# The first norm's sums of squares, taken along the turned tokens instead of by channel

## The chip, the cores and the metric

The kernel runs on one core of one Trainium2 chip. The metric is the device time of one execution in microseconds (us), the median of several. A core has TensorE (PE, with its weight loads shown apart as PEld), VectorE (DVE), ScalarE (ACT), GpSimd (POOL) and SyncE (SP), which here issues all transfers. Each engine runs its own instructions in order; between engines they wait on semaphores.

## The reference

A two-layer diffusion transformer over 512 latent and 256 context tokens of 1024 channels. Layer 0 mixes tokens by pooling, layer 1 by attention; both are followed by a squared-ReLU MLP. The change touches only the first norm, of layer 0:

```python
def rms_norm(x, g):
    xf = x.astype(jnp.float32)
    y = xf * lax.rsqrt(jnp.mean(xf * xf, axis=-1, keepdims=True) + EPS)
    return (y * g.astype(jnp.float32)).astype(x.dtype)
...
        a_l = modulate(rms_norm(h_lat, norm_g[i, 0]), sh1, sc1)
            a_c = modulate(rms_norm(h_ctx, norm_g[i, 0]), csh1, csc1)
            y_l = pool_mix(a_l, pool_w[j], pool_scale[j])
```

So for each of the 768 tokens a sum of 1024 squares is needed, then its inverse root, before the token can be pooled with its neighbours. The vectors sh1 and sc1 come from a product of the conditioning vector with `ada_w`, a weight of 24 MB per layer.

## The kernel before, in words

The tokens lie in memory with channels on the 128 partitions: `h_lat` (8 channel tiles x 512 tokens) and `h_ctx` (8 x 256). Both arrive as four pairs of channel tiles, latent and context in turn (lines 100 to 102). Behind them on SP's one queue come four 512 KB pieces of `ada_w` (`praw`, block 2), the pool weights `pw` (1 MB), four more pieces (`w`, block 4; lines 112 to 116), and then, as buffers come free, the pieces of the other blocks.

Lines 584 to 607 are the first norm. For each pair of channel tiles PE turns the tokens (transposes, L591) into PSUM; ACT copies the latent half (L597) and DVE the context half (L594) into `turned_m_hi` and `turned_m_lo`, where tokens lie on partitions. Next to that, and independent of it, ACT squares the unturned `h_lat` and `h_ctx` (`squares`, L263 and L266) and DVE adds the squares up by channel tile (L267). When all eight tiles are in, `rstd_cols` (lines 276 to 287) lets PE add over the partitions by products with a column of ones (L282), first for the latents, then for the context. DVE turns the sums into a variance (L284), POOL raises it to the power -0.5 (L286). Last, ACT and DVE scale three of the six turned token tiles each (L605, L607).

PE's order is written by hand from line 582 on. Behind the norm stand, in this order: `ada0_products(2)` (L187, on `praw`), the first pooled tile (L627, on the scaled tokens), `ada0_done(2)` (transposes L196, on ACT's copy L190 of the products), the second pooled tile, `ada0_products(4)` (L187 again, on `w`), the third pooled tile, `ada0_done(4)`, the fourth pooled tile and the first products of the pooling mixer (`mix`, L654). `ada0_done(2)` yields the scale `am` (DVE, L199 to L155), which ACT needs for `scaled` (L638); on ACT follow the rounding of `pw` (L86) and L190 of block 4. The order of ACT and DVE in this stretch is chosen by the framework's scheduler, until line 702.

After about 100 us the MLPs and the attention follow, for the rest of the time; nothing in them is edited.

Of the kernel before, what the change touches and what calls it, by code (L numbers as in the profile page):

```python
# [8 lines left out]
F32 = mybir.dt.float32  # L9
F32R = mybir.dt.float32r  # L10
AF = mybir.ActivationFunctionType
ALU = mybir.AluOpType
AX = mybir.AxisListType

P = 128
D = 1024
# [10 lines left out]
EPS = 1e-6  # L27
# [20 lines left out]
def dit_block_kernel(ctx: ExitStack, tc: tile.TileContext, xT, cols, adab, adaw, w1, w2, wqkv, wo,  # L48
                     poolw, gvec, rope, edge, eye, out):
    nc = tc.nc  # L50
    act, dve, pool, pe = nc.scalar, nc.vector, nc.gpsimd, nc.tensor

    def sb(stack, name, bufs):
        return stack.enter_context(tc.tile_pool(name=name, bufs=bufs))
# [6 lines left out]
    sc = sb(ctx, "sc", 4)  # L61
    sm = sb(ctx, "sm", 4)
# [11 lines left out]
    def new(p, shape, dt, tag, bufs=None):  # L74
        uid[0] += 1
        kw = {"bufs": bufs} if bufs else {}
        return p.tile(shape, dt, tag=tag, name=f"{tag}{uid[0]}", **kw)

    def ps_mm():
        return new(mm, [P, 1024], F32, "mm")  # L80

    def ps_aux():
        return new(aux, [P, 512], F32, "aux")
# [38 lines left out]
    neghalf = const.tile([P, 8], F32, tag="neghalf", name="neghalf")  # L122
# [117 lines left out]
    def hs(k0, k1, c0, n):  # L240

        if c0 < SEQ:
            return h_lat[:, k0:k1, c0 : c0 + n]
        return h_ctx[:, k0:k1, c0 - SEQ : c0 - SEQ + n]
# [14 lines left out]
    def squares(acc, k, w, c0, n, place=None, eng=dve):  # L259

        if acc is None:
            acc = new(accp[0], [P, w, n], F32, accp[1]) if place is None else place
            act.activation(acc, hs(k, k + w, c0, n), AF.Square)  # L263
        else:
            sq = new(sc, [P, w, n], F32, "sc")
            act.activation(sq, hs(k, k + w, c0, n), AF.Square)  # L266
            eng.tensor_tensor(acc, acc, sq, op=ALU.add)  # L267
        return acc
# [7 lines left out]
    def rstd_cols(n, accs, ps):  # L276

        m = n // P
        sums = [acc[:, j] for acc in accs for j in range(acc.shape[1])]
        for i in range(m):  # L280
            for j, x in enumerate(sums):
                pe.matmul(ps[:, i : i + 1], x[:, i * P : i * P + P], ones[:, :1], start=j == 0, stop=j == len(sums) - 1)  # L282
        var = new(sm, [P, m], F32, "sm8")
        dve.tensor_scalar(var, ps[:, :m], 1.0 / D, EPS, op0=ALU.mult, op1=ALU.add)  # L284
        rr = new(sm, [P, m], F32, "sm8")
        pool.tensor_tensor(rr, var, neghalf[:, :m], op=ALU.pow)  # L286
        return rr
# [291 lines left out]
    segs = ((0, 0, SEQ), (1, SEQ, CTX))  # L579
# [2 lines left out]
    by_hand.enter_context(tc.manual_schedule(engines={mybir.EngineType.PE}))  # L582

    turned = [big.tile([P, 4, D], F32, tag=t, name=f"turned_{t}") for t in ("m_hi", "m_lo")]
    accs = [None, None]
    for k in range(0, KT, 2):
        for s, c0, n in segs:
            ps = ps_aux() if s else ps_mm()
            for i in range(n // P):
                for kk in range(2):  # L590
                    pe.transpose(ps[:, i * 256 + kk * P : i * 256 + kk * P + P], hs(k + kk, k + kk + 1, c0 + i * P, P)[:, 0], ident)  # L591
            dst, src = turned[s][:, : n // P, k * P : k * P + 256], ps.rearrange("p (i c) -> p i c", c=256)
            if s:
                dve.tensor_copy(dst, src)  # L594
                accs[s] = squares(accs[s], k, 2, c0, n)
            else:
                act.activation(dst, src, AF.Copy)  # L597
                for kk in range(2):
                    accs[s] = squares(accs[s], k + kk, 1, c0, n)
    for s, c0, n in segs:  # L600
        rr = rstd_cols(n, [accs[s]], ps_aux())
        for i in range(n // P):
            t = turned[s][:, i]
            if i % 2:
                act.activation(t, t, AF.Copy, scale=rr[:, i : i + 1])  # L605
            else:
                dve.tensor_scalar(t, t, rr[:, i : i + 1], None, op0=ALU.mult)  # L607

    pooled = {}

# [35 lines left out]
    accs = [None, None]  # L646
# [217 lines left out]
    kk = kvp.tile([P, 2, NKV, T], F32R, tag="k", name="k")  # L864
# [3 lines left out]
    scale = HD ** -0.5  # L868
# [186 lines left out]
    for n in range(8 * NKV):  # L1055
        g, half, i = n // 8, n // 4 % 2, n % 4
# [140 lines left out]
```

## Time and profile before

| | us |
|---|---|
| median of 3 runs | 1263.3 (1262.46 to 1263.8) |
| the profiled execution | 1262.69 |
| its span, first to last instruction | 1260.7 |
| first transposes start | 6.13 |
| last transposes end | 15.04 |
| last scaled tile done (L605) | 23.86 |
| first product of the mixer (L654) starts | 33.15 |

The page gives busy time by engine (PE is busy in 98% of the span), the span in 40 slices, the transfer queues, the chain of work that ended last, and the costliest groups of instructions. The timeline of a stretch lists instructions in order of time: start, duration, engine, line, operation, output<-input, form and count, and in brackets the idle time before it with what ended it. The windows view gives busy time, granted TensorE clock (1.00 is full) and the share of the transfer engines for stretches of one's choice.

### The profile page before, as it was taken

What the parts mean: (1) busy time and instruction counts of PE and PEld (TensorE: products, weight loads), DVE (VectorE), ACT (ScalarE), POOL (GpSimd) and SP (SyncE); (2) the same over time, 40 slices, a digit from 0 to 9 for tenths busy, and PEclk for the clock granted to TensorE, in tenths of its full rate; (3) what the DMA queues carried; (4) which work ended last, traced back from release to release, by engine and by line L of the source; (5) the groups of instructions that cost most, each with busy time, mean ns of one, the idle gap of its engine ahead of it and who ended that gap; (6) DMA issues with size and microseconds to landing.
All of it is one profiled execution on the core that took longest, in us unless ns stands there. A gap on an engine that the chain in (4) does not pass through costs nothing.

```text
span 1260.7 us, 20578 instructions
## 1 busy us (share of the span) xinstructions
PE 1233.3 (98%) x8182; PEld 1105.2 (88%) x8182; DVE 1026.6 (81%) x1756; ACT 591.9 (47%) x1058; POOL 137.2 (11%) x130
## 2 busy tenths in 40 slices
PE   6999999999999999999999999999999999999997
PEld 5767888899999999999988899999988898989996
DVE  6664999778989888866788388879899989898976
ACT  6555523443444444333455255546555454545443
POOL 0300000122122322231012000000000000000002
PEclk8999999999999999999999999999999999999998
DMA  9766424333433333311122021212213232323101
GB/s 347 304 258 211 140 84 138 113 117 118 151 106 133 131 118 116 135 68 34 35 93 74 27 68 35 68 35 68 101 65 119 102 116 86 116 87 115 68 33 67
DMA packets 41311, 138.67 MB, mean 110 GB/s; under 512 B 4736, under 2 KB 8064, under 8 KB 41088
## 3 DMA queue, kind: packets, MB, share of 16 engines
q1 hardware_dynamic: 41216, 137.36, 30.8%
q8 instruction: 64, 1.05, 0.3%
q14 instruction: 31, 0.25, 0.1%
HBM read 135.25 MB, written 2.10 MB: 109 GB/s over the span
## 4 chain that ended last, share of the span: by engine, by line
PE 65%; issue 27%; DVE 5%; ACT 1%; POOL 1%; DMA 1%; SPq 0%; POOLq 0%; DVEq 0%; ACTq 0%
PE mm L490 10%; PE aux L490 10%; PE aux L877 8%; PE mm L371 6%; PE aux L459 5%; PE mm L439 5%; PE aux L439 4%; PE aux L1003 3%; PE aux L991 2%; PE aux L187 2%; PE mm L955 1%; PE aux L978 1%; PE mm L654 1%; PE mm L750 1%; DVE h_lat L348 1%
## 5 line engine op out<-in xcount | busy, mean ns | idle before, releaser
L490 PE MATMUL mm<-act,w 128*128 128x512 f32 (+1 forms) x1224 | 237.6, 345 | 1.8 <-DVE h_lat L348 1.8
L490 PE MATMUL aux<-act,w 128*128 128x512 f32 (+1 forms) x1224 | 238.9, 346 | 0.2
L490 PEld LDWEIGHTS mm<-act,w 128*128 128x128 f32 x1224 | 195.1, 189 | 32.7 <-DVE h_lat L348 2.0
L490 PEld LDWEIGHTS aux<-act,w 128*128 128x128 f32 x1224 | 194.9, 189 | 29.4 <-DVE h_lat L348 0.6
L87 DVE TENSOR_TENSOR w<-raw,w 128x1024 fp32r<-128x1024 f32 x106 | 129.4, 1225 | 31.8 <-ACT w L86 31.5
L86 ACT ACTIVATE w<-raw 128x1024 fp32r<-128x1024 f32 x106 | 110.2, 1055 | 78.7 <-PE aux L490 38.1
L348 DVE SCALAR_TENSOR_TENSOR h_lat<-aux,mod,h_lat 128x512 f32<-128x512 f32 (+1 forms) x204 | 126.6, 630 | 16.3 <-PE aux L490 14.7
L428 POOL TENSOR_TENSOR sc<-pair 128x512 f32<-128x512 f32 x55 | 76.7, 1403 | 320.3 <-DMA raw<-in_dram 106.8
L348 DVE SCALAR_TENSOR_TENSOR h_lat<-mm,mod,h_lat 128x512 f32<-128x512 f32 (+1 forms) x140 | 97.9, 701 | 6.1 <-PE mm L490 4.2
L371 PE MATMUL mm<-m_m_hi,w 128*128 128x512 f32 (+1 forms) x320 | 92.9, 352 | 0.1
L877 PE MATMUL aux<-w,a_m_hi 128*128 128x256 f32 (+1 forms) x384 | 86.4, 320 | 0.0
L219 DVE SCALAR_TENSOR_TENSOR mc<-raw,s_f,mc 128x512 f32<-128x512 f32 x112 | 84.0, 768 | 1.4 <-DMA raw<-in_dram 0.6
L439 PE MATMUL mm<-m_m_hi,mc 128*128 128x256 f32 x384 | 71.0, 283 | 0.0
L877 PEld LDWEIGHTS aux<-w,a_m_hi 128*128 128x128 f32 x384 | 63.4, 190 | 4.9
L459 PE MATMUL aux<-m_c,w 128*128 128x256 f32 x528 | 65.2, 283 | 0.0
L371 PEld LDWEIGHTS mm<-m_m_hi,w 128*128 128x128 f32 x320 | 56.1, 189 | 10.1 <-ACT r L379 0.8
L459 PEld LDWEIGHTS aux<-m_c,w 128*128 128x128 f32 x528 | 64.2, 192 | 0.0
L877 PE MATMUL aux<-w,a_m_lo 128*128 128x256 f32 (+1 forms) x192 | 61.2, 319 | 0.0
L439 PEld LDWEIGHTS mm<-m_m_hi,mc 128*128 128x128 f32 x384 | 60.7, 192 | 0.5
L286 POOL TENSOR_TENSOR sm<-sm,neghalf 128x2 f32<-128x2 f32 (+1 forms) x11 | 8.9, 811 | 466.6 <-DVE sm L284 466.6
L371 PE MATMUL mm<-m_m_lo,w 128*128 128x512 f32 (+1 forms) x160 | 55.9, 351 | 0.0
L439 PE MATMUL mm<-m_m_lo,mc 128*128 128x256 f32 x192 | 54.3, 283 | 0.0
(250 smaller groups left out, 2490.2 us busy)
## 6 DMA issues: line engine op xcount, KB each, us to landing
raw<-in_dram SPq DMA_DIRECT2D x155, 512.0 KB, 3.3
praw<-in_dram SPq DMA_DIRECT2D x34, 512.0 KB, 7.3
fin<-in_dram SPq DMA_DIRECT2D x24, 512.0 KB, 4.1
pair<-in_dram SPq DMA_DIRECT2D x22, 512.0 KB, 4.4
block<-in_dram SPq DMA_DIRECT2D x8, 512.0 KB, 7.6
h_lat<-in_dram SPq DMA_DIRECT2D x4, 512.0 KB, 6.4
w<-in_dram SPq DMA_DIRECT2D x4, 512.0 KB, 10.7
out_dram<-fin SPq DMA_DIRECT2D x8, 256.0 KB, 2.2
```

Of the source, the lines that this page charges most:

```text
L86: act.activation(hi, src, AF.Copy)
L87: lo_eng.tensor_tensor(lo, src, hi.bitcast(F32), op=ALU.subtract)
L187: pe.matmul(ps[o : o + P // CG, :512], s_w[:, kt], t[:, kk * 512 : kk * 512 + 512], start=kt < CG, stop=kt >= KT - CG)
L219: dve.scalar_tensor_tensor(acc[:, s], w, scal, acc[:, s], op0=ALU.mult, op1=ALU.add)
L348: dve.scalar_tensor_tensor(h, ps, gate[:, dt, s : s + 1], h, op0=ALU.mult, op1=ALU.add)
L371: pe.matmul(ps[:, c0 : c0 + cn], lhs, ms(m, ax, k, c0, cn), start=k + wx + ax == 0, stop=k == KT - 1 and wx == 1)
L428: eng.tensor_tensor(t, x, y, op=how)
L439: pe.matmul(places[n], w[:, wx, k * P : k * P + P], inputs[n][ax][:, k], start=k + wx + ax == 0, stop=k == 3 and wx == 1)
L459: pe.matmul(pc[:, t * 256 : t * 256 + 256], ws[k // 4][:, wx, k % 4 * P : k % 4 * P + P], ms(m, ax, k, SEQ, CTX), start=k + wx + ax == 0, ...
L490: pe.matmul(ps, lhs, a[:, t, ax, c0 : c0 + n], start=t + wx + ax == 0, stop=t == 1 and wx == 1)
L877: pe.matmul(ps, lhs, ws[u][:, wx, o : o + width], start=k + ax + wx == 0, stop=k == KT - 1 and ax == 1)
L1003: pe.matmul(ps[:, :256], ws[j][:, wx, dt * P : dt * P + P], o[:, ax, j], start=j + wx + ax == 0, stop=j == 1 and ax == 1)
```

## The change

The squares are no longer taken from the unturned `h_lat` and `h_ctx`. After the second and the fourth pair of channel tiles, that is for each half of 512 channels, the six turned token tiles are squared and summed along their own 512 elements in one instruction each: ACT takes the three odd ones (`Square` with `accum_out`), DVE the three even ones (`tensor_tensor_reduce`). Each gives one column of `sums`. Then DVE adds the two halves and makes the variance of all six tiles, POOL raises it once, and the scaling is as before. The adds L267, the products with ones L282 and the separate treatment of latents and context go.

```diff
-    accs = [None, None]
+    sums = new(sm, [P, 2, 6], F32, "sums", 1)
     for k in range(0, KT, 2):
         for s, c0, n in segs:
...
             if s:
                 dve.tensor_copy(dst, src)
-                accs[s] = squares(accs[s], k, 2, c0, n)
             else:
                 act.activation(dst, src, AF.Copy)
-                for kk in range(2):
-                    accs[s] = squares(accs[s], k + kk, 1, c0, n)
-    for s, c0, n in segs:
-        rr = rstd_cols(n, [accs[s]], ps_aux())
-        for i in range(n // P):
-            t = turned[s][:, i]
-            if i % 2:
-                act.activation(t, t, AF.Copy, scale=rr[:, i : i + 1])
-            else:
-                dve.tensor_scalar(t, t, rr[:, i : i + 1], None, op0=ALU.mult)
+        if k % 4 == 2:
+            for i in range(6):
+                x = (turned[0][:, i] if i < 4 else turned[1][:, i - 4])[:, k * P - 256 : k * P + 256]
+                sq, ss = new(sc, [P, 512], F32, "sc"), sums[:, k // 4, i : i + 1]
+                if i % 2:
+                    act.activation(sq, x, AF.Square, accum_out=ss)
+                else:
+                    dve.tensor_tensor_reduce(sq, x, x, 1.0, 0.0, op0=ALU.mult, op1=ALU.add, accum_out=ss)
+    var = new(sm, [P, 6], F32, "sm8")
+    dve.tensor_tensor(var, sums[:, 0], sums[:, 1], op=ALU.add)
+    dve.tensor_scalar(var, var, 1.0 / D, EPS, op0=ALU.mult, op1=ALU.add)
+    rr = new(sm, [P, 6], F32, "sm8")
+    pool.tensor_tensor(rr, var, neghalf[:, :6], op=ALU.pow)
+    for i in range(6):
+        t = turned[0][:, i] if i < 4 else turned[1][:, i - 4]
+        if i % 2:
+            act.activation(t, t, AF.Copy, scale=rr[:, i : i + 1])
+        else:
+            dve.tensor_scalar(t, t, rr[:, i : i + 1], None, op0=ALU.mult)
```

From line 599 on, lines of the new kernel stand up to nine higher: L605 becomes L614, L607 becomes L616, L627 becomes L636, L638 becomes L647. L187, L190 and L196 keep their numbers.

PE's order before, from the last transposes of the context (`aux_291`) to the first pooled tile (`mm_341`); `aux_300` and `aux_313` are the sums over partitions, `aux_330` the products of ada block 2:

```order
L591 MATMUL aux_291<-ident,h_ctx 128x128 x4
L282 MATMUL aux_300<-ones,mc_212 128x1 x4
L282 MATMUL aux_313<-ones,mc_223 128x1 x4
L187 MATMUL aux_330<-praw_112,s_w_148 32x512 x2
L187 MATMUL aux_330<-praw_113,s_w_148 32x512 x2
L187 MATMUL aux_330<-praw_114,s_w_148 32x512 x2
L187 MATMUL aux_330<-praw_115,s_w_148 32x512 x2
L627 MATMUL mm_341<-bands,turned_m_hi 128x129 x3
```

And the same place now, with `aux_273` for the last transposes, `aux_308` for the products and `mm_319` for the pooled tile:

```order
L592 MATMUL aux_273<-ident,h_ctx 128x128 x4
L187 MATMUL aux_308<-praw_112,s_w_148 32x512 x2
L187 MATMUL aux_308<-praw_113,s_w_148 32x512 x2
L187 MATMUL aux_308<-praw_114,s_w_148 32x512 x2
L187 MATMUL aux_308<-praw_115,s_w_148 32x512 x2
L636 MATMUL mm_319<-bands,turned_m_hi 128x129 x3
```

The products of ada block 2 now stand directly behind the transposes; the rest of PE's order is the same.

DVE's order before, from the third copy of turned context tokens (`aux_266`) to the scaling; `mc_212` and `mc_223` are the running sums by channel, `sm` the variances and inverse roots:

```order
L594 COPY turned_m_lo<-aux_266 128x2x256
L267 TENSOR_TENSOR mc_212<-mc_212,sc_263 128x512
L267 TENSOR_TENSOR mc_223<-mc_223,sc_272 128x512
L125 COPY mod_135<-bcol 128x96
L267 TENSOR_TENSOR mc_212<-mc_212,sc_285 128x512
L594 COPY turned_m_lo<-aux_291 128x2x256
L267 TENSOR_TENSOR mc_212<-mc_212,sc_288 128x512
L267 TENSOR_TENSOR mc_223<-mc_223,sc_297 128x512
L284 TENSOR_SCALAR sm_305<-aux_300 128x4
L284 TENSOR_SCALAR sm_318<-aux_313 128x2
L607 TENSOR_SCALAR turned_m_hi<-turned_m_hi,sm_307 128x1024 x2
L607 TENSOR_SCALAR turned_m_lo<-turned_m_lo,sm_320 128x1024
```

And now, from the third copy (`aux_257`); an ISA row with `sc` is a `tensor_tensor_reduce`, the ISA row behind it reads its accumulator into `sums_202`:

```order
L595 COPY turned_m_lo<-aux_257 128x2x256
L125 COPY mod_135<-bcol 128x96
L595 COPY turned_m_lo<-aux_273 128x2x256
L605 ISA sc_279,sums_202<-turned_m_hi 128x512
L605 ISA sums_202 128x1
L605 ISA sc_283,sums_202<-turned_m_hi 128x512
...
L605 ISA sc_287,sums_202<-turned_m_lo 128x512
...
L607 TENSOR_TENSOR sm_291<-sums_202 128x6
L608 TENSOR_SCALAR sm_291<-sm_291 128x6
L616 TENSOR_SCALAR turned_m_hi<-turned_m_hi,sm_294 128x1024 x2
L616 TENSOR_SCALAR turned_m_lo<-turned_m_lo,sm_294 128x1024
```

Six instructions that square and read out now stand between DVE's last copy and the variance, where two adds stood; ACT likewise has three squares behind its last copy, where two stood. Past this place DVE, ACT, POOL and SP run the same instructions in the same order as before.

## The prediction

> **What bounds the kernel now.** I read the page first, then the chain of waits in the first 36 us, then the timeline there, then the transfers. The slices of the page, 31.5 us each, show that the first one is unlike the rest:
>
> ```profile
> PE   6999999999999999999999999999999999999997
> DMA  9766424333433333311122021212213232323101
> ```
>
> PE is full from the second slice on and nothing after the norm is edited, so the change can act only in the first slice, where PE has gaps and the transfer engines are full. The chain of waits there (start, duration, work):
>
> ```profile
> 17.37 3.58 PE aux L282 x16
> 20.95 3.33 PE aux L187 x16
> 24.28 1.53 PE mm L627 x12
> 25.81 0.45 PE aux L196 x4
> 26.97 1.99 ACT act L638 x4
> 28.97 1.89 ACT w L86 x2
> 30.86 0.50 ACT sc L190
> 31.40 0.66 PE aux L196 x4
> 33.40 2.11 PE mm L654 x12
> ```
>
> The sums over partitions (L282) hold PE for 3.58 us; the products of ada block 2 (L187) queue behind them; with those done come the first pooled tile, the transposes L196 and, through `am`, ACT's work, until the mixer starts. From there on PE is dense. So the gain is what L654 moves forward.
>
> **The tail after the last transposes.** The timeline of this stretch, all engines:
>
> ```profile
> 10.61 1.02 ACT L597 ACTIVATE turned_m_hi<-mm 128x1024 f32<-128x1024 f32 x1
> 13.54 1.06 PE L591 MATMUL mm<-ident,h_lat 128*128 128x128 f32 x8 [0.62 <-ACT turned_m_hi L597]
> 14.44 0.60 PE L591 MATMUL aux<-ident,h_ctx 128*128 128x128 f32 x4
> 15.01 1.01 ACT L597 ACTIVATE turned_m_hi<-mm 128x1024 f32<-128x1024 f32 x1
> 16.03 0.68 DVE L594 COPY turned_m_lo<-aux 128x512 f32<-128x512 f32 x1
> 16.43 0.62 ACT L266 ACTIVATE sc<-h_ctx 128x512 f32<-128x512 f32 x1
> 16.63 1.28 DVE L267 TENSOR_TENSOR mc<-mc,sc 128x512 f32<-128x512 f32 x2
> 19.28 0.16 DVE L284 TENSOR_SCALAR sm<-aux 128x4 f32<-128x4 f32 x1 [1.36 <-PE aux L282]
> 19.59 1.01 POOL L286 TENSOR_TENSOR sm<-sm,neghalf 128x4 f32<-128x4 f32 x1 [18.68 <-DVE sm L284]
> 20.63 2.19 ACT L605 ACTIVATE turned_m_hi<-turned_m_hi,sm 128x1024 f32<-128x1024 f32 x2 [3.58 <-POOL sm L286]
> 22.73 1.13 ACT L605 ACTIVATE turned_m_lo<-turned_m_lo,sm 128x1024 f32<-128x1024 f32 x1
> 24.38 0.60 ACT L190 ACTIVATE sc<-aux 128x512 f32<-128x512 f32 x1 [0.52 <-PE aux L187]
> ```
>
> The reduce on DVE does not occur before. Its nearest rows: an elementwise product's twin, the add L267, of the same size; the three-operand product L219, also with two sources in SBUF; and the accumulator read that ACT's squares of the attention need:
>
> ```profile
> L267 DVE TENSOR_TENSOR mc<-mc,sc 128x512 f32<-128x512 f32 x9 | 5.9, 687 | 0.5 <-ACT sc L266 0.4
> L219 DVE SCALAR_TENSOR_TENSOR mc<-raw,s_f,mc 128x512 f32<-128x512 f32 x112 | 84.0, 768 | 1.4 <-DMA raw<-in_dram 0.6
> L884 ACT ACTIVATION_READ_ACCUMULATOR sc<-aux 128x1 f32 x8 | 1.7, 207 | 0.0
> ```
>
> Lower end 0.64 us (half of L267's 1.28 for two, the read hidden), upper end 0.77 + 0.21 = 0.98; I take 0.85, 0.69 for the product and 0.16 for the read, a small DVE instruction like L284. A first use that costs more has no row and goes into a rival. DVE's last copy can start when the transposes end, 14.44 + 0.60 = 15.04, and ends at 15.75 (now 16.71, behind adds). Three reduces: 15.8 + 3 x 0.85 = 18.35 (17.7 to 18.7). ACT is not later: its last copy moves from 15.01 to 14.65, when the latent transposes are done, and the three squares of 0.62 to 0.82 end at 17.6 to 18.2. The first half's reduces cost nothing: DVE is free for them from ACT's second copy, 10.61 + 1.02, on, and 11.7 + 3 x 0.85 + 0.9 for two copies is 15.15, just in time; without that cover each 0.1 us on a reduce would count six times, not three.
>
> Add and variance, two small dependent instructions of 0.16 and a hand-over each: 18.35 + 0.4 = 18.75. POOL follows 0.15 us behind (19.28 + 0.16 to 19.59) with 1.0 us: 19.9. The scaling on ACT, three in a row at about 1.05 us apart and 1.13 for the last, runs 19.95 to 23.2. Now the last ends at 22.73 + 1.13 = 23.86. So the norm itself gains only **0.66 us**: two pipelined half norms become one, and all six tiles wait for it.
>
> **PE no longer stands in between.** L282's 3.58 us go, and L187 of block 2 starts as its pieces land:
>
> ```profile
> L108 SPq DMA_DIRECT2D praw<-in_dram x4: 328/328/520, 7.2 to 11.3; - x4
> DMA to landing us min/median/max: 8.1/8.1/8.4
> ```
>
> 7.2 + 8.4 = 15.6 to 11.3 + 8.1 = 19.4; with the last quarter behind it, at most 3.33 / 4 = 0.83 us, it is over at 20.3 instead of 24.28. It is then hidden behind the scaling. The first pooled tile ends with the last scaled tile, about 23.6. ACT's L190 comes directly behind the scaling, 23.2 to 23.8. L196 can start at 23.85 instead of 25.65 or so (25.81 in the chain): **1.8 us** earlier, and `am` and L638 with it, 26.97 to 25.15.
>
> **What is late next.** The products of ada block 4, the next L187 in PE's order, and block 3 behind it for comparison; the issue of the third and the last piece of block 4 on SP's queue with their times to landing; PE's weight loads at the end of the block:
>
> ```profile
> 27.52 2.11 PE L187 MATMUL aux<-w,s_w 128*32 128x512 f32 x16
> 35.43 1.92 PE L187 MATMUL aux<-praw,s_w 128*32 128x512 f32 x16
> 28.40 0.31 PEld L187 LDWEIGHTS aux<-w,s_w 128*32 128x32 f32 x6 [0.31 <-issue]
> ```
>
> ```profile
> 14.53 0.43 SPq L116 DMA_DIRECT2D w<-in_dram  x1
> w<-in_dram SPq DMA_DIRECT2D x1, 512.0 KB, 11.2
> 15.57 0.33 SPq L116 DMA_DIRECT2D w<-in_dram  x1
> w<-in_dram SPq DMA_DIRECT2D x1, 512.0 KB, 13.0
> ```
>
> The third piece lands at 14.53 + 11.2 = 25.7, the last at 15.57 + 13.0 = 28.6. That is in the middle of the block as it now runs: the last loads go on until 28.40 + 0.31 = 28.71, and the block takes 2.11 where block 3 takes 1.92. PE meets this piece already today. The windows say why it can't come sooner by itself:
>
> ```profile
> 17.08:23.91 6.83, 6.54 (x32) 0.50 1.02 412
> 23.91:30.70 6.79, 6.79 (x58) 1.00 1.03 407
> ```
>
> The transfers run at 100% and some 410 GB/s, SP's order is unchanged, and no buffer that PE frees earlier lies ahead of this piece. With PE 1.8 us early, it waits. Behind the landing only the last quarter is left, 28.6 + 0.45, so the third pooled tile starts at 29.05 instead of 29.6: 0.5 us. ACT's L190 of block 4 follows at 29.2 (ACT is through with L638 and L86 at 30.86 - 1.8 = 29.05), so the 0.3 us by which L196 now waits for it (31.10 to 31.40: 29.6 + 1.5 for the tile) goes too. L654 starts about **0.7 us** earlier; bounds are 0.3, where only ACT's wait goes, and 1.0, where the piece lands 0.2 sooner as well. The other 1.1 us of the 1.8 are spent waiting for the last piece of block 4.
>
> The clock enters in the same place. The row above shows the granted clock at 0.50 from 17.08 to 23.91, while PE did little, and 1.00 after L187's dense 3.33 us. After the change PE is sparser until 23.6, so it may need another such stretch at half the clock: L196 and the second pooled tile, 0.45 + 1.5 us at full clock, then take about 3.9 and end near 27.5, still ahead of 28.6. Either way the landing decides.
>
> [...]
>
> Sum against the profiled execution: 1262.69 - 0.7 = 1262.0 (its span 1260.7, 2.0 us lie around it). It stands 0.6 below the median of 1263.3, so on the median the forecast is 1263.3 - 0.7 = **1262.6**.
>
> **Rivals.** *The last piece lands on time.* Between the landings of the third and the last piece lie 2.9 us; 1.3 would be the pace of 512 KB at 410 GB/s. In that gap a fetch of instructions ran on the same engines:
>
> ```profile
> q8 instruction: 1, 0.02, 33.8%
> ```
>
> That is the transfer view of 26.0 to 26.2 us: 33.8% of 16 engines for 0.2 us is 1.08 us on one of them. PE has 32 instructions fewer ahead of this point (L282's 16 products and 16 loads), so the fetch moves by 32 of PE's instructions, which is from L196 to the beginning of block 4's products: some 25.8 to 27.5, about where it was. If it falls clear, the piece lands at 27.0, the full 1.8 us come through at full clock, and the time is 1261.5. For it: the gap is an accident of one engine. Against: the place hardly moves.
>
> *The reduce is slow.* If writing an accumulator doubles DVE's time, 2 x 0.77 + 0.2 = 1.74 us, six of them lie end to end: 11.7 + 6 x 1.74 + 1.6 for the copies = 23.7 instead of 18.35, and everything behind is 5.35 us later: L196 at 29.2, 3.55 later than now, past any wait for the transfer. The time is 1263.3 + 3.5 = 1266.8. It decides from about 1.13 us per reduce, where L196 comes when it comes now; 0.2% is lost from 1.55. For it: no row shows a reduce with accumulator. Against: L219, with the same two sources, runs at 0.77.
>
> [...]
>
> *A milder loss.* A reduce of 1.2 to 1.4 us, or a PE that stays slow beyond 27.5, costs 0 to 1.8 us: up to 1265.1.
>
> [...]
>
> **How the numbers follow.** Forecast 0.55, landing on time 0.20, milder loss 0.13, slow reduce 0.07, the gate on top 0.05. A measurement of this kernel tells about 0.2%, 2.5 us, from no change. Only the gate case is faster by that, 0.05; only the slow reduce slower, 0.07; the rest is within, 0.88. The range takes in the first three cases, 1261.5 to 1265.1, with a little below for the spread of the runs: 1261.0 to 1265.1, leaving out 0.12.
>
> **What would show it.** No L282 before 60 us; L187 on `praw` from 15.6 to about 20; the reduces at about 0.85 with their read; the last scaled tile near 23.2; L196 near 23.9; then PE idle inside L187 on `w`, with the last piece landing near 28.6; L654 at 32.2 to 32.9 instead of 33.15. Wrong would be: reduces over 1.1 us, L654 at or behind 33.15, or block 4's products over by 28.2.

## The result, and the profile after

The changed kernel takes 1254.49 us, the median of 6 runs (1252.93 to 1254.87), against 1262.26 us before (6 runs, 1261.42 to 1263.8): a ratio of 0.9935 [0.9923, 0.9947], some 8 us faster where 0.7 was forecast. The profiled execution took 1254.56 us with a span of 1252.4, 8.3 below the span before.

The first norm does most of what the forecast said of it. The timeline of the changed kernel behind the last transposes (start, duration, engine, line, count, and in brackets what ended an idle stretch; L605 and the accumulator read are DVE's reduce, L610 is POOL's root, L614 ACT's part of the scaling):

```profile
9.57 1.97 PE L592 MATMUL mm<-ident,h_lat 128*128 128x128 f32 x8 [0.71 <-DMA h_lat<-in_dram]
15.63 0.60 PE L592 MATMUL aux<-ident,h_ctx 128*128 128x128 f32 x4
16.16 2.10 PE L187 MATMUL aux<-praw,s_w 128*32 128x512 f32 x8
16.89 0.69 DVE L605 CUSTOM_DVE_ANT_0 sc<-turned_m_hi 128x512 f32<-128x512 f32 x1
17.51 0.08 DVE L605 DVE_READ_ACCUMULATOR2_ANT sums<- 128x1 f32 x1
17.51 0.69 DVE L605 CUSTOM_DVE_ANT_0 sc<-turned_m_hi 128x512 f32<-128x512 f32 x1
19.44 1.32 POOL L610 TENSOR_TENSOR sm<-sm,neghalf 128x6 f32<-128x6 f32 x1 [18.53 <-DVE sm L608]
19.77 1.05 PE L187 MATMUL aux<-praw,s_w 128*32 128x512 f32 x4 [0.23 <-DMA praw<-in_dram]
22.90 1.13 ACT L614 ACTIVATE turned_m_lo<-turned_m_lo,sm 128x1024 f32<-128x1024 f32 x1
24.56 0.66 PE L196 MATMUL aux<-ident,sc 128*128 128x128 f32 x4
26.49 2.92 PE L187 MATMUL aux<-w,s_w 128*32 128x512 f32 x16
28.36 0.14 PEld L187 LDWEIGHTS aux<-w,s_w 128*32 128x32 f32 x4 [0.87 <-DMA w<-in_dram]
32.48 0.83 PE L663 MATMUL mm<-act,w 128*128 128x512 f32 x3
```

L282 is gone, block 2's products run from 16.16 to 20.82 as their pieces land, and PE then waits inside block 4's for the last piece. The mixer's first product (L654 before, L663 now) starts at 32.48. The same product stood at 33.15 before, so the norm's share in this pair of profiles is 0.67 us.

The rest has to be looked for behind it. A way to see where is to follow the start of the same instruction through both traces: the mixer's first product, the first product of new weights on `m` (L750 before, L759 after), and four of the later sums over partitions (L282), which neither kernel changes. Before:

```profile
33.15 1.18 PE L654 MATMUL mm<-act,w 128*128 128x512 f32 x5
76.62 0.50 PE L750 MATMUL mm<-m_m_hi,w 128*128 128x512 f32 x1 [0.51 <-ACT m_m_hi L734]
616.66 1.05 PE L282 MATMUL mm<-ones,mc 128*128 128x1 f32 x8
640.18 0.95 PE L282 MATMUL mm<-ones,act 128*128 128x1 f32 x8
892.72 1.05 PE L282 MATMUL mm<-ones,mc 128*128 128x1 f32 x8
1239.03 0.50 PE L282 MATMUL mm<-ones,ss 128*128 128x1 f32 x4
```

After:

```profile
74.33 0.50 PE L759 MATMUL mm<-m_m_hi,w 128*128 128x512 f32 x1 [0.50 <-ACT m_m_hi L743]
609.52 1.05 PE L282 MATMUL mm<-ones,mc 128*128 128x1 f32 x8
634.52 0.94 PE L282 MATMUL mm<-ones,act 128*128 128x1 f32 x8
886.09 1.05 PE L282 MATMUL mm<-ones,mc 128*128 128x1 f32 x8
1231.30 0.50 PE L282 MATMUL mm<-ones,ss 128*128 128x1 f32 x4
```

The lead is 0.67 us, then 2.29, 7.14, 5.66, 6.63 and 7.73. Two kinds of step make it. The jumps, 1.62 us forward up to 76 us and 1.48 back between 617 and 640, belong to the granted clock: stretches at half of it (0.50 and 0.51 below), which the text calls shut windows or a shut gate, stand elsewhere than before. The windows of the changed kernel (length, busy time of PE, PEld, DVE, ACT, POOL, then granted clock, DMA share, GB/s):

```profile
68.30:71.70 3.40, 3.40 (x32) 2.03 (x24) 0.31 (x2) 0.60 (x1) 0.32 (x1) 1.00 1.03 412
625.70:629.10 3.40, 3.40 (x17) 3.40 (x17) 2.22 (x6) 1.55 (x3) 0.00 (x0) 0.51 0.50 174
888.60:892.00 3.40, 3.40 (x18) 3.40 (x18) 2.43 (x6) 2.63 (x6) 0.00 (x0) 0.50 0.00 0
```

Before, the first of these stretches was the one at 0.50, and the other two stood at 1.00. The first and the one ahead of it, before (length, busy time of PE, granted clock, DMA share, GB/s):

```profile
64.90:68.30 3.40, 3.05 (x29) 1.00 1.04 419
68.30:71.70 3.40, 3.40 (x21) 0.50 1.02 407
```

The third costs 0.8 us (the lead falls from 6.6 to 5.8 between 893 and 900). Together the gate gives 1.62 and takes 1.48 and 0.8: it is not the gain.

The other kind is a steady growth: 4.85 us from 76 to 617 us, 1.0 from 640 to 893 and 1.9 from 900 to 1239, 7.8 in all. PE has hardly a gap there and runs the same products in the same order. They are shorter. The groups with the largest change, before (count, then busy us and mean ns; PEld is the load of weights):

```profile
L459 PE MATMUL aux<-m_c,w 128*128 128x256 f32 x528 | 65.2, 283 | 0.0
L459 PEld LDWEIGHTS aux<-m_c,w 128*128 128x128 f32 x528 | 64.2, 192 | 0.0
L439 PE MATMUL mm<-m_m_hi,mc 128*128 128x256 f32 x384 | 71.0, 283 | 0.0
L439 PE MATMUL aux<-xs,h_ctx 128*128 128x256 f32 x288 | 36.5, 283 | 0.0
```

and after:

```profile
L459 PE MATMUL aux<-m_c,w 128*128 128x256 f32 x528 | 61.6, 276 | 0.0
L459 PEld LDWEIGHTS aux<-m_c,w 128*128 128x128 f32 x528 | 60.8, 188 | 0.0
L439 PE MATMUL mm<-m_m_hi,mc 128*128 128x256 f32 x384 | 69.8, 281 | 0.0
L439 PE MATMUL aux<-xs,h_ctx 128*128 128x256 f32 x288 | 35.9, 279 | 0.0
```

In the raw starts, 489 of 517 steps from one L459 product to the next were 120 ns before, and all are 113 or 114 ns after. That is 3.5 of the 7.8 us in one line that the edit does not touch.

What the edit does touch is memory. The new tile `sums`, 48 bytes a partition rounded up to 64, is a buffer of its own in the pool `sm`. In the two built programs every buffer of SBUF, the core's working memory, that is allocated behind it lies 64 bytes further: of the ring that holds `m_c`, the buffer at 154656 now begins at 154720, and likewise the buffers of `mc`, `raw`, `praw`, `xs`, `op`, `k`, `v`, `fin`. What is allocated ahead of it stays: `h_lat`, `h_ctx`, the big `m_hi` and `m_lo`, `w`, `act`, `r`, `sc`. L459 multiplies a tile that moved, `m_c`, by one that did not, `w`. Before, both began at 32 modulo 256 bytes in a partition (a buffer of `w`, for one, at 76832); now `m_c` begins at 96.

### The profile page after: what moved, and what is told of

Its sections match the earlier page's. It is cut to its first block, busy times and chain, and to the rows that moved or that the text cites. A ratio compares the mean times of both kernels' runs of the same rounds, so it can differ in the third digit from the quotient of the medians.

```text
span 1252.4 us, 20540 instructions
## 1 busy us (share of the span) xinstructions
PE 1225.9 (98%) x8166; PEld 1096.9 (88%) x8166; DVE 1024.7 (82%) x1758; ACT 589.4 (47%) x1058; POOL 137.8 (11%) x129
## 4 chain that ended last, share of the span: by engine, by line
PE 63%; issue 27%; DVE 5%; DMA 2%; ACT 1%; POOL 1%; SPq 0%; POOLq 0%; DVEq 0%; ACTq 0%
PE mm L490 10%; PE aux L490 10%; PE aux L886 8%; PE mm L371 6%; PE mm L439 5%; PE aux L459 5%; PE aux L439 4%; PE aux L1012 3%; PE aux L1000 2%; PE mm L964 1%; PE aux L987 1%; PE mm L759 1%; PE aux L187 1%; DVE h_lat L348 1%; PE mm L663 1%
## 5 line engine op out<-in xcount | busy, mean ns | idle before, releaser
L490 PE MATMUL mm<-act,w 128*128 128x512 f32 (+1 forms) x1224 | 238.5, 346 | 1.8 <-DVE h_lat L348 1.8
L490 PE MATMUL aux<-act,w 128*128 128x512 f32 (+1 forms) x1224 | 239.2, 346 | 0.3
L490 PEld LDWEIGHTS mm<-act,w 128*128 128x128 f32 x1224 | 195.7, 190 | 32.9 <-DVE h_lat L348 2.0
L490 PEld LDWEIGHTS aux<-act,w 128*128 128x128 f32 x1224 | 195.1, 189 | 29.6 <-DVE h_lat L348 0.7
L371 PE MATMUL mm<-m_m_hi,w 128*128 128x512 f32 (+1 forms) x320 | 92.6, 351 | 0.1
L439 PE MATMUL mm<-m_m_hi,mc 128*128 128x256 f32 x384 | 69.8, 281 | 0.0
L371 PEld LDWEIGHTS mm<-m_m_hi,w 128*128 128x128 f32 x320 | 56.1, 189 | 9.9 <-ACT r L379 0.8
L459 PE MATMUL aux<-m_c,w 128*128 128x256 f32 x528 | 61.6, 276 | 0.0
L459 PEld LDWEIGHTS aux<-m_c,w 128*128 128x128 f32 x528 | 60.8, 188 | 0.0
L439 PEld LDWEIGHTS mm<-m_m_hi,mc 128*128 128x128 f32 x384 | 59.4, 188 | 0.5
L371 PE MATMUL mm<-m_m_lo,w 128*128 128x512 f32 (+1 forms) x160 | 55.8, 350 | 0.0
L439 PE MATMUL mm<-m_m_lo,mc 128*128 128x256 f32 x192 | 53.9, 281 | 0.0
```

Source lines behind the costliest of these rows:

```text
L371: pe.matmul(ps[:, c0 : c0 + cn], lhs, ms(m, ax, k, c0, cn), start=k + wx + ax == 0, stop=k == KT - 1 and wx == 1)
L439: pe.matmul(places[n], w[:, wx, k * P : k * P + P], inputs[n][ax][:, k], start=k + wx + ax == 0, stop=k == 3 and wx == 1)
L459: pe.matmul(pc[:, t * 256 : t * 256 + 256], ws[k // 4][:, wx, k % 4 * P : k % 4 * P + P], ms(m, ax, k, SEQ, CTX), start=k + wx + ax == 0, ...
L490: pe.matmul(ps, lhs, a[:, t, ax, c0 : c0 + n], start=t + wx + ax == 0, stop=t == 1 and wx == 1)
```

## The experiments

### Shift without the norm, norm without the shift

Four kernels on one chip, beside 24 runs of the kernel before at 1263.75 us. Three keep the old norm and add an unused tile to the same pool (16, 32 or 8 floats: 64, 128 or 32 bytes):

```diff
     accs = [None, None]
+    pad = new(sm, [P, 16], F32, "pad", 1)
+    pool.memset(pad, 0.0)
```

The fourth has the new norm, with its sums in a ring of 64-byte buffers that is there already, so that nothing moves:

```diff
-    sums = new(sm, [P, 2, 6], F32, "sums", 1)
+    sums = new(sm, [P, 2, 6], F32, "sm16", 2)
```

*Old norm, 64 bytes.*

> The old norm, with nothing but an unused 64-byte tile (set to zero once, on POOL) where the new norm has its tile of sums. Every buffer allocated behind it, the ring of m_c and of the mixer's operands, the raw weights and the Strassen tiles among them, moves up by 64 bytes per partition, as in the changed kernel. Placement theory (PE's products run faster when the moving operand and the weights do not have the same address modulo 128 bytes): the products L459 go from 120 to about 113 ns start to start, and the time drops by some 4 to 7 us, to about 1257, though the first 33 us stay as they were. Theory of the norm (the gain comes from the norm's own instructions and what follows from them): no change, 1262. Theory of the rotation (the new norm takes two fewer buffers of the mc ring, so later tiles fall on other buffers): no change, 1262.

Measured: 1255.31 us (1254.27 to 1256.55), 0.9936 [0.9924, 0.9949]. The unused tile alone gives what the whole change gave. Its trace has the mixer's first product where it was, the same gain in the middle, and none of the norm; the last line is L459's group, 65.2 us before:

```profile
33.16 2.21 PE L656 MATMUL mm<-act,w 128*128 128x512 f32 x11
611.51 1.05 PE L282 MATMUL mm<-ones,mc 128*128 128x1 f32 x8
1231.21 0.50 PE L282 MATMUL mm<-ones,ss 128*128 128x1 f32 x4
L459 PE MATMUL aux<-m_c,w 128*128 128x256 f32 x528 | 61.8, 276 | 0.0
```

*New norm, nothing moved.*

> The new norm, with its sums in a buffer of a ring that is there already (48 of 64 bytes), so that no later buffer moves. Placement theory: the 0.7 us at the mixer's start are kept and the rest is gone, 1261 to 1262, L459 back at 120 ns. Theory of the norm, and of the rotation, which is as in the changed kernel: all of it is kept, 1254.5, L459 at 113 ns.

Measured: 1260.78 us (1259.06 to 1263.16), 0.998 [0.997, 0.9989]. The norm by itself gains 2.5 us (1.4 to 3.8 by the interval), more than 0.7. In its profile the products take what they took before (L459 is at 65.2 us again); the lead of 2.2 us at the mixer grows to 3.8 where the gate stays open at 68, and then stays at 3.5 to 3.8 to the end:

```profile
30.94 2.36 PE L663 MATMUL mm<-act,w 128*128 128x512 f32 x12
612.93 1.05 PE L282 MATMUL mm<-ones,mc 128*128 128x1 f32 x8
1235.49 0.50 PE L282 MATMUL mm<-ones,ss 128*128 128x1 f32 x4
L459 PE MATMUL aux<-m_c,w 128*128 128x256 f32 x528 | 65.2, 283 | 0.0
```

The four tiles of `m_c` take the buffers of their ring in the same order here as in the changed kernel, and in another order than before. That alone gains nothing in L459, so the theory of the rotation falls too.

*Old norm, 128 bytes.*

> The old norm with an unused tile of 128 bytes at the same place. If the address modulo 128 decides: no change, 1262, L459 at 120 ns. If any move of the buffers does it (another row, another distance to what the other engines use): as with 64 bytes, about 1257.

Measured: 1260.09 us (1257.98 to 1262.54), 0.9974 [0.9964, 0.9983]. Not the same as no shift, so 128 bytes is not the period. L459 takes 64.4 us, and 1.4 us of this profile's lead are the norm's, with one stretch at half clock instead of two.

*Old norm, 32 bytes.*

> The old norm with an unused tile of 32 bytes at the same place. If operands have to be 64 bytes apart modulo 128: no change, 1262. If any difference modulo 128 is enough, or modulo 64: as with 64 bytes or part of it, 1257 to 1260.

Measured: 1258.38 us (1256.1 to 1260.89), 0.9963 [0.995, 0.9976], L459 at 63.4 us: 64% of the 64 bytes' gain (5.4 of 8.4 us below the 1263.75), and half of what L459 had.

### The place of one tile, or the distance between two

Four more with the old norm, beside 11 runs of before at 1263.05 us. The edit puts 64 bytes ahead of the weights' pool, behind it, or both (here behind it):

```diff
     wp = sb(ctx, "wp", 4)
+    g1 = sb(ctx, "g1", 1).tile([P, 16], F32, tag="g1", name="g1")
+    pool.memset(g1, 0.0)
     ap_ = sb(ctx, "ap", 2)
```

*Ahead of the weights: `w` and `m_c` both moved by 64.*

> The old norm; 64 bytes per partition are put ahead of the weights' pool, so that the weights, act, m_c, op and xs all lie 64 bytes further and only h_lat, h_ctx and the big m_hi/m_lo tiles stay. Theory A (a 256-wide product is slower, 119 to 120 ns from start to start, where its moving tile and its weights lie at the same place modulo 128 bytes, and 113 to 118 ns where they lie 64 apart): L459 (m_c with w, both moved) stays at 119 to 120 ns, so its 3.3 us are not gained; L439 (m_m_hi with op or mc, xs with h_ctx: one of the two moved) gains its 0.8 us in layer 0 and 1.8 us in layer 1; about 1260, ratio 0.998. Theory B (what counts is where the later tiles lie by themselves, against what the other engines write beside the products): L459 falls to 113 to 114 ns as with the 64 bytes behind sm; about 1255.5, ratio 0.9936.

Measured: 1257.89 us (1255.73 to 1259.78), 0.9958 [0.9946, 0.997]. The lines are those of theory A, and the time is 2 us below its 1260. L459 (two lines further down here) is back at the old duration although both its tiles have moved, and L439 with `w`, of which one has moved, gains for the first time (33.6 us before):

```profile
L461 PE MATMUL aux<-m_c,w 128*128 128x256 f32 x528 | 65.2, 283 | 0.0
L441 PE MATMUL mm<-m_m_hi,w 128*128 128x256 f32 x176 | 32.4, 278 | 0.0
```

*Ahead and behind: `w` by 64, the later tiles by 128.*

> The old norm; 64 bytes ahead of the weights' pool and 64 more behind it: modulo 128 the weights alone have moved, all else lies where it lay (the later tiles 128 bytes further). Theory A: L459 (m_c with w) falls to 113 to 114 ns and gains 3.3 us, L439 stays at 120 (op, xs, mc with m_m_hi and h_ctx as before); about 1259, ratio 0.9970. Theory B: L459 stays at 119 to 120; what is gained is at most what the shift of 128 bytes gained (0.9974), and not in L459 beyond its 0.8 us.

Measured: 1258.05 us (1255.58 to 1259.85), 0.9963 [0.9951, 0.9975]. L459 has its full gain from the other side, and L439 with `mc` has none:

```profile
L463 PE MATMUL aux<-m_c,w 128*128 128x256 f32 x528 | 61.6, 276 | 0.0
L443 PE MATMUL mm<-m_m_hi,mc 128*128 128x256 f32 x384 | 71.0, 283 | 0.0
```

These two settle it for the pairs of L459 and L439: the distance between a product's two tiles counts, not the place of either.

*Behind: all but `w` by 64.*

> The old norm; 64 bytes behind the weights' pool: act, r, sc and all that comes later move by 64 bytes, the weights stay. Against the 64 bytes behind sm only act, r and sc have moved besides. Theory A: L459 113 to 114 ns and L439 as there, 1255.3 (0.9936), and L490 (act with w, 512 wide) shows whether a wide product gains too: none by the mixed pairs seen so far (233 ns against 232). Theory B: the same L459; L490 may move by 1 to 3 us either way, since what ACT and DVE write (act, r, sc) has moved.

Measured: 1252.46 us (1251.58 to 1257.63), 0.9924 [0.991, 0.9937], the fastest layout. L459 is at 61.6, and the 512-wide products of `act` with `w` (L490 and L654 before), of which `act` alone has moved, have not gained: from one start to the next they take 231.0 ns before and 230.9 here, the mean of 1344 steps. A wide product shows no gain. But layer 1's L439 gains three times as much as with the shift behind `sm`, though its own two tiles are as far apart as there:

```profile
L441 PE MATMUL mm<-m_m_hi,mc 128*128 128x256 f32 x384 | 67.5, 277 | 0.0
L441 PE MATMUL aux<-xs,h_ctx 128*128 128x256 f32 x288 | 34.6, 276 | 0.0
```

Only `act`, `r`, `sc` and the small tiles of `sm` have moved besides, so a third tile seems to have a part in it; and with `w` moved too (the run ahead of the weights) the first of these groups is at 69.8, as behind `sm`. How was not tried.

*192 bytes behind `sm`.*

> The old norm with 192 bytes behind sm, which is 64 modulo 128. Theory A: the same as 64 bytes, 1255.3, ratio 0.9936, L459 113 to 114 ns. Theory B (the place itself, with a longer period than 128 bytes): another time, between 1255 and 1262, with other lines moved, as the 128 bytes moved L490 by 2.6 us and L459 by only 0.8.

Measured: 1254.11 us (1253.8 to 1256.59), 0.9939 [0.9926, 0.9951]. The time is that of 64 bytes, as theory A had it, and the lines are not: L459 has a third of its gain, and the attention's L991 (two lines further down here, 37.9 before, 36.8 with 64 bytes) more than its own. None of these three profiles has a shut window within L991; the changed kernel's has one, at 889, and shows 37.8. So A is right on the distance and wrong on its period.

```profile
L459 PE MATMUL aux<-m_c,w 128*128 128x256 f32 x528 | 64.0, 281 | 0.0
L993 PE MATMUL aux<-act,v 128*128 128x256 f32 x288 | 36.5, 279 | 0.1
```

*256 bytes behind `sm`.*

> The old norm with 256 bytes behind sm. If only the distance modulo 256 counts (0: slow, 64: fast, 128 and 192: between): as before, L459 at 120 ns, 1262 to 1263, ratio 0.999 to 1.000. If the period is longer: L459 at 115 to 118 ns as with 128 and 192, ratio 0.994 to 0.998.

Measured: 1263.42 us (1259.61 to 1266.61), 0.9997 [0.9983, 1.0011], beside 29 runs of before at 1263.21. As before, and not only in the sum: L459, L439, L991 and L1003 have the busy times of before to 0.1 us. So the distance counts modulo 256, as far as one multiple of it can show.

```profile
L459 PE MATMUL aux<-m_c,w 128*128 128x256 f32 x528 | 65.2, 283 | 0.0
L439 PE MATMUL mm<-m_m_hi,mc 128*128 128x256 f32 x384 | 71.0, 283 | 0.0
```

By how far `m_c` lies behind `w` modulo 256, L459's 528 products then take:

| distance, bytes | 0 | 32 | 64 | 128 | 192 |
|---|---|---|---|---|---|
| busy, us | 65.2 | 63.4 | 61.6 to 61.8 | 64.4 | 64.0 |

This is L459's curve alone. L439's `m_m_hi` with `mc`, 71.0 us at 0, takes 70.1, 69.8, 71.2 and 69.8 with 32, 64, 128 and 192 bytes behind `sm`.

### What the norm itself gains

*Block 2 first, in the old norm.* One part of the change alone:

```diff
+    row = ada0_products(2)
     for s, c0, n in segs:
         rr = rstd_cols(n, [accs[s]], ps_aux())
...
-    row = ada0_products(2)
     tile0 = pool_tile(0)
```

> The old norm with one part of the change alone: the products of block 2 (L187 on praw) stand ahead of the sums over partitions (L282) on PE, so PE works as the pieces land from 15.5 on instead of idling until 17.4. Theory D (the idle stretch of 2.3 us ahead of L282 is what lets the clock gate shut for one or two windows of 3.4 us behind it): the clock stays open from its first opening through the norm, L654 starts at 31.5 to 32.5 though the sums come later, ratio 0.998 to 0.9995. Rival (the gate answers to something else): one or two windows are shut between 17 and 26 us as before, the sums end near 23 and L654 starts at 33.5 or later, ratio 1.000 to 1.001.

Measured: 1265.42 us (1263.76 to 1268.75), 1.0011 [0.9999, 1.0024], beside the same 29 runs of before at 1263.21. Theory D fails as put: the idle stretch is gone, and the gate shuts all the same for two windows, now from 22.61 on, behind the stretch that holds L282, and L654 starts at 34.94. The columns are those of the windows above:

```profile
19.20:22.61 3.41, 2.98 (x22) 2.01 (x20) 0.32 (x2) 0.60 (x1) 0.76 (x1) 1.00 0.99 398
22.61:26.03 3.42, 2.24 (x10) 2.26 (x10) 2.08 (x3) 3.14 (x4) 1.07 (x2) 0.51 1.04 414
26.03:29.44 3.41, 3.41 (x17) 3.30 (x17) 1.51 (x4) 2.67 (x4) 0.00 (x0) 0.50 1.02 404
```

PE counts as busy for 2.98 us in the stretch ahead of it, 1.95 of them products of one column each (L282). What shuts the gate is not shown by this run, and the scheduler also exchanged a few instructions of ACT and DVE in this kernel.

*The weights of block 4 ahead of `pw`, in the new norm with nothing moved.*

```diff
-    pw = pp.tile([P, KT, 256], F32, tag="pw", name="pw")
-    nc.sync.dma_start(pw, poolw.rearrange("p (k n) -> p k n", k=KT))
     for u in range(0, 4, 2):
...
             nc.sync.dma_start(pair[:, x], adaw[0, 4, u + x])
+    pw = pp.tile([P, KT, 256], F32, tag="pw", name="pw")
+    nc.sync.dma_start(pw, poolw.rearrange("p (k n) -> p k n", k=KT))
```

> The new norm without the shift (sums in a ring that exists already), and the four pieces of block 4 (w) are sent for ahead of pw, so that they land 2.5 us earlier and pw last. If the transfer of w is what ends the norm's gain (forecast, step e): L187 on w no longer waits, takes 1.9 us instead of 2.8 to 2.9, and L663 starts about 1 us earlier than in the run with pw first (30.9 and 32.5 so far), ratio 0.997. Rival: pw, now last, holds the next step: its split by ACT and DVE comes late and L663 starts at 32 or later, no gain over 0.998.

(The step of the forecast that is meant is "What is late next".)

Measured: 1262.8 us (1260.83 to 1265.36), 0.9992 [0.9981, 1.0004]: the rival. With the transfers in another order, the scheduler also ordered some later instructions of PE, ACT and DVE differently. Block 4's products no longer wait, and the mixer waits for ACT's and DVE's split of `pw` instead, which landed last:

```profile
24.98 1.92 PE L187 MATMUL aux<-w,s_w 128*32 128x512 f32 x16
31.50 0.97 PE L663 MATMUL mm<-act,w 128*128 128x512 f32 x4 [1.27 <-ACT w L86]
32.76 1.66 PE L663 MATMUL mm<-act,w 128*128 128x512 f32 x8 [0.29 <-DVE w L87]
```

*The new norm in the fastest layout* (its sums in the ring, and the 64 bytes behind the weights' pool).

> The new norm with its sums in a ring that exists already (nothing moves by it), and 64 bytes behind the weights' pool, so that act, r, sc and all later tiles lie 64 bytes further. Theory A (two gains that are independent of each other: the norm's 2.5 us as in the run without the shift, and the distance of 64 bytes between moving tile and weights, 10.6 us with act, r and sc moved too): 1263.05 - 2.5 - 10.6 = about 1250, ratio 0.990. Theory C (the gains overlap, the shift being what helps the norm too): 1252.5, as with the old norm.

Measured: 1252.39 us (1251.74 to 1254.2), 0.9907 [0.9889, 0.9926]; by the medians, taken on different chips, it beats the changed kernel by 2 us and is level with the old norm in this layout. The median is theory C's; the interval of the ratio holds A's 0.990 as well as C's 0.992, so this run does not decide between them. The mixer starts 0.70 us earlier than with the old norm there (31.68), but this execution has a shut window at 627 which the other has not, worth 1.5 us (from 611 to 634 us its lead of 1.1 turns into 0.4 behind):

```profile
30.98 2.24 PE L665 MATMUL mm<-act,w 128*128 128x512 f32 x11
```

*The changed kernel and the old norm with 64 bytes, side by side on one chip.*

> The changed kernel itself, beside the old norm with the same shift of 64 bytes, on one chip. If the new norm adds its 0.7 us of L663 and the shut windows it saves (2.5 us without the shift) to the shift's gain: 2 to 2.5 us below the old norm with the shift, ratio 0.9915 against 0.9935. If the shut windows turn up elsewhere (at 626 and 889 us as in its first profile): 0 to 1 us below, ratio 0.993 to 0.9935.

> The old norm with 64 bytes behind sm, beside the changed kernel on one chip: 0.9935 again, L656 near 33.2 or 31.8 us by two or one shut windows in the norm.

Measured: 1254.86 us (1253.0 to 1256.64), 0.9939 [0.9923, 0.9955], and 1256.46 us (1254.89 to 1257.1), 0.995 [0.9933, 0.9966], beside 11 runs of before at 1262.65. The new norm adds 1.6 us to the shift by the medians, between the two cases that were put, and the intervals overlap. In the two profiles the mixer starts at 31.07 and 31.73, 0.66 us apart.

## Why the prediction was wrong, and where it was right

**The step that failed** is its first: "nothing after the norm is edited, so the change can act only in the first slice", and "From there on PE is dense. So the gain is what L654 moves forward." PE is dense there, and its instructions are unchanged. That was taken to mean that their durations are unchanged. They are not: the new tile moves every buffer behind it by 64 bytes, and products that read a moved and an unmoved tile become shorter (L459 from 65.2 to 61.6 us, L439's `m_m_hi` with `mc` from 71.0 to 69.8), 7.8 us in all. The forecast had put this term at nothing. The old norm with an unused tile has the whole of it (0.9936), the new norm without the move has none of it (L459 at 65.2 us). The edit's line `sums = new(sm, ...)` was in the diff; what it does to the addresses of others was not asked. No rival held this.

**The norm's own steps**, against the trace:

- *The reduce.* Forecast 0.85 us with its read, 0.64 to 0.98. Measured 0.69 for the product and 0.08 for the read, which overlap: 0.61 from one to the next. The slow reduce did not come: no run shows the doubled time, 1.74 us, from which that rival was added up. This reduce, with an accumulator and with one fp32 tile in SBUF as both of its sources, takes 0.69 us, as long as the plain add of the same size (687 ns). No run here has a reduce over two different tiles.
- *The norm's tail.* Forecast: last scaled tile at 23.2 instead of 23.86. Measured 22.90 + 1.13 = 24.03, for two reasons outside the reduce. The transposes ended at 16.23 and not 15.04: the second pair of latents landed late in this execution (9.57 against 8.79), and the clock was late too (the eight transposes of the third pair still took 1.91 us, from 12.19 on, where before they took 1.06, from 11.43 on). And POOL's root took 1.32 us on six columns, not 1.0. In the profile of the new norm with nothing moved the same tile ends at 21.47 + 1.13 = 22.60. The cover of the first half's reduces held, although two copies on DVE take 1.2 us (0.61 each to the next instruction) and not the 0.9 of that sum, which the slow-reduce rival put at 1.6.
- *L282's time and block 2.* Right: no L282, products from 16.16 to 20.82 (forecast 15.6 to 20.3). L196 came at 24.56, not 23.85, by the late transposes.
- *What is late next.* Right: PE waits 0.87 us for the last piece of block 4, and starts again at 28.36 (forecast 28.6). The run with the pieces in the other order shows that this wait is not the only one: without it `pw` is late.
- *The mixer.* Forecast 0.7 us earlier, measured 0.67 here, 0.70 and 0.66 in the two pairs of profiles with equal layouts. That the 0.67 comes so near is in part luck: in that pair the new norm's transposes ended 1.2 us late, and the old norm had two shut windows where the other two pairs had one.
- *The clock in the norm.* "it may need another such stretch at half the clock": it needed none. (The row that this rested on has PE busy for 6.54 of 6.83 us, so "while PE did little" misreads it; what the timeline shows is 2.33 us of idleness ahead of L282, and then products of one column.) Between the clock's first opening and 34 us none of the five profiles of the new norm has a shut window, and all eleven of the old norm have one or two. This is where the norm's gain can exceed 0.7: over the profiles with the old norm in its own order the mixer starts between 31.44 and 33.80, mean 32.4 (10 profiles), and with the new norm between 30.94 and 32.48, mean 31.4 (the 4 with `pw` first). So the direction was right and the size, 0.7, is near 1.0 on the mean. The 2.5 us measured without the move include shut windows elsewhere: its four runs with a granted clock of 0.997 average 1259.2 us, its three with 0.993 1263.0, and the ten of the kernel before with 0.993, on the same chip, 1263.1.
- *The gate at 68.* The chances give 0.05 to "the gate on top", a full clock from 68.3 us on, where it was 0.50 before. No run shows what decides that, so this was the author's estimate. In this execution the stretch did stand at 1.00, worth 1.62 us, and two other windows were shut, at 626 and 889, which no rival had. In the second profile of the changed kernel 68 is shut again.

What stays open: why a distance of 64 bytes modulo 256 is cheap and 0 dear (61.6 and 65.2 us for L459), why L459 gains more than the other pairs in the changed kernel, and which third tile, if it is one, moves layer 1's L439. All would need products timed alone. How much of the norm's own gain is left once the layout is chosen is open too: 1.6 us with overlapping intervals in one layout, level medians in the other.

## What to carry to other kernels

A new tile in a pool moves every buffer behind it, here by 64 bytes. When a kernel bound by PE gets faster or slower without a change in its dense stretch, compare the mean duration of unchanged products in the two profiles, then the addresses, and repeat the measurement with an unused tile of the same size and, the other way round, with the edit in a buffer that exists already. Only those two together say what the edit is worth. And where products of 256 columns fill PE, the distance between their two tiles is a thing to tune by itself: in this kernel it is worth 10.6 us of 1263.05 with an edit of two lines (the run with all but `w` moved by 64).

## What the runs showed of the hardware

**Two tiles of a product, 256 bytes.** The 528 products of L459 (256 columns, fp32r tiles) run at 120 ns from start to start with their two tiles at distance 0 modulo 256 bytes in a partition, and at 113 to 114 with 64; their loads of weights are shorter too (192 and 188 ns). Other 256-wide pairs gain less from the same 64 bytes in the changed kernel: `m_m_hi` with `mc` and `xs` with `h_ctx` go from 120 to 117 or 118 ns for most steps, `mc` with `w` from 119.6 to 117.7 on the mean; and `act` with `w` goes from 118.1 to 117.6 in the fastest layout. 512-wide products gained nothing: `act` with `w` as above, and the 192 products of `m_m_hi` and 96 of `m_m_lo` with `w` (L371 before) are at 68.7 and 37.9 us before and again where `w` alone of the two had moved (the run with 64 bytes ahead of the weights). In L459 the step from product to product depends on where the two tiles lie to each other, by 6 of 120 ns. By what way, no run here shows.

**The gate's windows.** Between the clock's first opening (at 10.25 us before, 14.76 in the changed kernel) and the program's last 10 us, the stretches at half clock last 3.4 us or twice that and begin at a slightly different time in each execution (behind the norm's L282 at 17.08 before and at about 20.4 with 128 bytes behind `sm`). They come behind stretches in which PE is idle for a part or runs products of one column: behind L282 in the norm, and at about 68, 626 and 889 us. In the changed kernel PE is busy for 1.59 of the 3.40 us ahead of the window at 626 and for 2.57 ahead of the one at 889, and in the kernel before for 3.05 of 3.40, most of them L282's, ahead of the one at 68. The changed kernel has the same 3.05 ahead of 68.30, and the clock stays at 1.00 there, so the traces do not show what decides it. One of them costs 0.8 to 1.6 us, and the profiles of the old norm differ by up to 2.4 us at the mixer (31.44 to 33.80), the late ones with two shut windows ahead of it, the early ones with one.

**A reduce with an accumulator**, of a tile with itself, costs DVE little more than a plain elementwise instruction of the size: 0.69 us and a read of 0.08 for 128 x 512 of fp32, where the add L267 takes 0.687.
